# A hybrid decoder step on one core: warm-up products, another order of the first loads, bias tables in steps, and output weights prepared before the turn

## The chip, the cores and the metric

The kernel runs on one core of a Trainium2 chip. The metric is the device time of one execution in microseconds (us), as the median of the runs shown. A profile is one execution recorded by the hardware profiler. Engines are named as in the profile: PE is TensorE's matmuls and PEld its weight loads, DVE is VectorE, ACT is ScalarE, POOL is GpSimd, SP is SyncE, which issues nearly all DMAs.

## What is computed

One layer of a decoder for 512 prompt tokens and 32 new sample tokens (8 sequences of 4), 2048 channels, all in float32. In short:

```python
h = rms_norm(x, norm_pre)
z = h @ w_in                      # 2048 x 7680: q, k, v, gate_attn, conv a, conv b, gate_conv
att_p = attend_prompt(q, k, v)    # 12 heads x 128, three dilated windows, one relative bias table
att_s = attend_sample(q, k, v, cache_kv)   # 8 sequences, 2048 cached rows each
c = pointwise(silu(layer_norm(depthwise_conv(a * sigmoid(b)))))
mix = concat(att * silu(gate_att), c * silu(gate_conv))
y = x + rms_norm(mix @ w_out, norm_post)   # 2048 x 2048
```

The outputs are y, the new convolution states, the prompt's k and v, and the whole key and value cache shifted by 4 rows with the new rows behind (some 200 MB that are copied from DRAM to DRAM).

## The kernel before

**Splitting.** Each large product is made of three products of a faster float type: a value is split into a high half (a cast on ACT) and a low half (value minus high half, on POOL or DVE), and high x high, low x high and high x low are summed. A weight half is called wh or wl for the input projection and owh or owl for the output projection, x is split into xh and xl, and the mix into mh and ml.

**Input projection.** 60 column tiles of 128 columns are taken in a fixed order, `order`; n counts them. The 544 tokens are two halves of 272, so a tile is 16 x 2 x 3 = 96 products, written by `mm` at L107 into banks z. `project` (L849) makes a tile in four parts; each part calls `split` (L798) for weights that come two quarters later, and `split` calls `load_w` (L149) two half tiles ahead, into four buffers `raw`. After each part comes a `tick` (L767). As each half of a tile is done, `out` (L989) multiplies it by the token scale R on DVE; the gates' tanh and products follow the tile (L1034).

**First tiles.** The first NF = 3 tiles are made together by `project_first` (L879), row by row as x arrives: `prepare` (L908) splits x rows (`split_x`, L252) and weights (`split_first`, L886) one quarter ahead. R needs the sum of squares of each token: `square` (L271) on ACT from a second copy of x by tokens (`load_xtok`, L268; five blocks, the fifth holds the 32 last tokens), then `token_rsqrt` (L195) on ACT and DVE, and a product with a diagonal (rbx) that spreads it. `make_R` (L312) stands ahead of the last six rows of products.

**Bias tables.** `make_tabs` (L295) makes the relative bias tables by four products (tb, rb) that share one bank `s`, each followed by an ACT copy; the first pair goes to DRAM (dtab) and is read back for each head by `load_toep`. It is a generator: each `yield` is a step.

**Side work.** Attention of the heads, the samples' work and the convolution are generators, `Side` (L60), that `tick` advances in order of their rank: a yield gives the ticks until the next step. For the samples a key unit takes UTK ticks and a value unit UTV ticks (L44); there are 24 of each, and each unit loads 1.75 MB of cache (kvf, kvm) into buffers of two. `tick` also sends pending stores (`flush_late`) and issues copies of the cache (`bulk`, L321) while the bytes sent are below START + PACE x the columns that PE has been given so far (L46, L775).

**Order.** Each engine runs its instructions in the order of the program (`in_order`, L76), and SP issues in that order too: a load that waits for its buffer holds what is behind it.

**The turn.** After tile 59 come the gate of the last head, the samples' last gate (`ms`, L1064), the closing of the attention buffers, loads of gpost (gp) and of the samples' x, and then `split_mix` (L779) for the mix rows 2 to 15 (rows 0 and 1 were made at n = 57). The output projection (L1146) takes four groups of 512 columns, 16 rows each; a row is 3 products of 512 columns for each of two token blocks. `split_out` (L821) splits the output weights up to 6 rows ahead, with low halves on POOL, every third on DVE. The 32 sample rows go another way: `sample_rows` (L1131) multiplies the unsplit weights in `oraws` by the samples' mix `smix` (os, L109), four rows at a time.

```python
            if n == NF - 1:
                project_first(first)
                add(make_tabs(), 0, 0)
                now[0] += 8
                for _ in range(4):
                    tick()
...
    ms = mixg[2][:, :, SEQ:]
    nc.vector.scalar_tensor_tensor(ms, ms, 0.5, smp["sg"], op0=ALU.mult, op1=ALU.mult)
    ap_.close()
...
    nc.gpsimd.tensor_copy(smix[:, 8:12, :], ms)
    for i in range(NPRE, KT):
        split_mix(i)
```

Of the kernel before, what the change touches and what calls it, by code (L numbers as in the profile page):

```python
# [10 lines left out]
F32 = mybir.dt.float32  # L11
# [7 lines left out]
P = 128  # L19
# [23 lines left out]

UTK, UTV = 3.8, 3.7  # L44

# [40 lines left out]
def body(tc, xT, xtok, gpost, w_in, w_out, ckv, cconv, relb, vecs, pww, c_oht, c_ohr, c_lmr, c_tm, c_pick,  # L86
# [88 lines left out]
    epsc = keep.tile([P, 1], F32, name="epsc")  # L175
    dma(vec, vecs)
    make_identity(nc, ident)
    nc.vector.memset(epsc, EPS)
# [10 lines left out]
    ones = keep.tile([P, P], F32, name="ones")  # L189
    nc.vector.memset(ones, 1.0 / 2048)  # L190

    sumsq = keep.tile([P, 5], F32, name="sumsq")
    nc.vector.memset(sumsq, 1.0)

    def token_rsqrt(ss, pool):  # L195


        r, v, w = [pool.tile([P, 5], F32, name=n + "x") for n in "rvw"]
        diag = pool.tile([P, 5, P], F32, name="diagx")
        nc.scalar.activation(r, ss, AF.Sqrt, bias=epsc[:, 0:1], scale=1.0 / 2048)  # L200
# [40 lines left out]
    def load_x(c):  # L241
        xr = ip.tile([P, 2, TOK], F32, tag="xr", name=f"xr{c}", bufs=6)
        if c:
            dma(xr, xT[:, 2 * c:2 * c + 2, :])
        else:
            for j in range(2):
                dma(xr[:, j, :], xT[:, j, :])
        return xr
# [14 lines left out]


    def xt_of(b):
        return mixg[(b + 1) % 4].rearrange("p a b -> p (a b)")[:P if b < 4 else NS, :D]

# [550 lines left out]
    osplits, oraws = {}, {}  # L818
    due = []

    def split_out(j):  # L821
# [24 lines left out]
        if j % 4 == 3:  # L846
            due.append(j - 3)

    def project(n, hi, lo, out):  # L849
# [29 lines left out]
    def project_first(outs):  # L879
# [28 lines left out]
        def prepare(c):  # L908
            if c == 0:
                split_x(0)  # L910
                ws = [split_first(0, n) for n in range(NF)]
                split_x(1)
            else:
                split_x(2 * c)
                ws = [split_first(c, n) for n in range(NF)]
                split_x(2 * c + 1)
            return ws

        ws = prepare(0)
        for c in range(4):  # L920
            nxt = prepare(c + 1) if c < 3 else None
            if c == 2:
                square(0)
                load_xtok(4)
                square(1)
            if c == 3:
                for b in range(2, 5):
                    square(b)
            rows(c, ws, 0, 2)
            if c < 3:  # L930
                rows(c, ws, 2, 4)
            ws_, ws = ws, nxt
# [6 lines left out]
    def samples():  # L939
        got = iter(())  # L940
        for g in range(3):
# [5 lines left out]
            state["vdone"] = g  # L947


    nc.scalar.activation(sumsq[:, 0:1], epsc, AF.Sqrt)  # L950
    load_w(0)
    xrs[0] = load_x(0)
    load_w(2)
# [8 lines left out]
    xrs[7] = load_x(7)  # L962
    for b in range(4):
        load_xtok(b)
# [4 lines left out]
    for n in range(N_IN):  # L969
        c = order[n]  # L970
        kind, h = divmod(c, NH)
        if n == NF:
            ini.close()
            sample_open()
            load_far(0)
            load_mid(0)
# [12 lines left out]
        def out(hf, z, t_=t_, c=c, g=g if c < 3 * NH else None, hh=hh if c < 3 * NH else None, nm=nm, n=n):  # L989
            if n == N_IN - 1 and hf == 0:  # L990
                for j in range(4):
                    split_out(j)
            if c >= NH:
# [8 lines left out]
        if n < NF:  # L1002
            first.append(out)
            if n == NF - 1:
                project_first(first)
                add(make_tabs(), 0, 0)
                now[0] += 8
                for _ in range(4):
                    tick()
        else:  # L1010
            project(n, xh, xl, out)
        if n == NF + 1:
            load_toep(0)
# [3 lines left out]
        if n == N_IN - 3:  # L1017
            smix = ring["a"].tile([P, KT, NS], F32, name="smix")
            for g in (0, 1, 3):
                nc.gpsimd.tensor_copy(smix[:, 4 * g:4 * g + 4, :], mixg[g][:, :, SEQ:])  # L1020
            for i in range(NPRE):
                split_mix(i)
        if n == NF:
            add(samples(), 0, 1)
# [50 lines left out]
    nc.gpsimd.tensor_copy(smix[:, 8:12, :], ms)  # L1075
    for i in range(NPRE, KT):
        split_mix(i)
    NBLK = 5
# [15 lines left out]
    def take_out(c, b, z):  # L1094
# [13 lines left out]
        nc.vector.tensor_tensor(ys[b][:np_, cs], z[:np_, :], gp[:np_, cs], op=ALU.mult)  # L1108

    def finish(b):  # L1110
        np_ = P if b < 4 else NS
# [16 lines left out]
    OLOOK = 6  # L1128
    sz = {}

    def sample_rows():  # L1131

        while due:
            j0 = due.pop(0)
            c = j0 // KT
            if c not in sz:
                sz[c] = bank("acc", f"os{c}")
            for a in range(4):
                i = (j0 + a) % KT
                mm(sz[c][a * NS:a * NS + NS, :], smix[:, KORD[i], :], oraws.pop(j0 + a).rearrange("p a b -> p (a b)"),  # L1140
                   start=(i < 4), stop=(i >= KT - 4), tile_position=(0, a * NS))
            if (j0 + 4) % KT == 0:
                take_out(c, 4, sz[c])

    sample_rows()
    for c in range(4):  # L1146
        last = c == 3

        for bs in (((0, 1), (2,), (3,)) if last else ((0, 1), (2, 3))):
            tags = ("z", "z") if 0 in bs else ("att", "s") if 2 in bs else ("t",)  # L1150
            z = [bank(t, f"oz{c}_{b}") for b, t in zip(bs, tags)]
            for i in range(KT):
                j = c * KT + i

                for a in range(OLOOK + 1):
                    if (j + a) // KT == c or 0 not in bs and j + a < NSLOT + c * KT + i:
                        split_out(j + a)
                        sample_rows()
                wh, wl = osplits[j]
                for b, z_ in zip(bs, z):  # L1160
# [139 lines left out]
```

## Time and profile before

| | |
|---|---|
| median of 3 runs | 1174.95 us (1173.05 to 1175.88) |
| profiled execution, its own time | 1170.97 us |
| span of the profile (first to last instruction) | 1169.2 us |
| PE busy | 1137.5 us, 97% |
| mean granted TensorE clock | 0.990 |
| moved by DMA | 401.92 MB, mean 344 GB/s |

Times in the profile count from the start of the span. A line of the timeline gives start, length, engine, source line, operation with the names of what it writes and reads, the number of merged instructions (x), and in brackets how long the engine was idle before and what ended that. Products in `mm` all have line 107, so they are told apart by names: z is the input projection, oz the output projection, os the samples' rows, tb and rb the tables, rbx the token scale.

### The profile page before, as it was taken

How to read it: one execution, taken by the hardware profiler on the slowest of the kernel's cores; microseconds unless marked ns; L12 is line 12 of the kernel's file. 1: busy time of each engine (PE TensorE's matmuls, PEld its weight loads, DVE VectorE, ACT ScalarE, POOL GpSimd, SP SyncE). 2: the span in 40 equal slices, each digit the busy share in tenths (PEclk: the TensorE clock that was granted, in tenths of full speed). 3: DMA queues.
4: the chain of work that ended last, by engine and by line, in shares of the span. 5: the costliest groups of instructions: out<-in, count | busy, mean ns of one | idle time of the engine just before them, and what ended most of it. 6: DMA issues, size and time to landing. Idle time of an engine off the chain costs nothing.

```text
span 1169.2 us, 23598 instructions
## 1 busy us (share of the span) xinstructions
PE 1137.5 (97%) x9322; PEld 1029.4 (88%) x9322; DVE 674.0 (58%) x1997; ACT 378.1 (32%) x749; POOL 406.8 (35%) x353
## 2 busy tenths in 40 slices
PE   7899999999999999999999999999999999999996
PEld 7699999999999999999999999899999976776775
DVE  5209899599699988778233576994222243112136
ACT  5433333422123332331334333423222253223241
POOL 5043323344344333333322222334333445313130
PEclk9989999999999999999999999999999998999999
DMA  9899999999998998999998899889999968999966
GB/s 363 278 339 373 402 351 343 383 312 338 408 329 320 402 381 323 351 362 355 408 375 331 293 384 395 330 317 373 387 386 338 337 218 292 337 357 389 332 232 225
DMA packets 96083, 401.92 MB, mean 344 GB/s; under 512 B 15000, under 2 KB 17816, under 8 KB 89765
## 3 DMA queue, kind: packets, MB, share of 16 engines
q1 hardware_dynamic: 95972, 400.42, 93.6%
q8 instruction: 73, 1.20, 0.4%
q14 instruction: 38, 0.30, 0.1%
HBM read 388.65 MB, written 212.66 MB: 514 GB/s over the span
## 4 chain that ended last, share of the span: by engine, by line
PE 56%; DVE 2%; DMA 1%; issue 1%; POOL 0%; ACT 0%; SPq 0%; DVEq 0%; ACTq 0%; POOLq 0%
PE z L107 32%; PE oz L107 14%; PE o L109 3%; PE pwp L107 1%; PE os L109 1%; PE att L107 1%; DMA raw<-in_w_out_dram 1%; PE s L107 1%; PE t L113 1%; DVE qsc L628 1%; POOL owl L844 0%; PE kt L113 0%; PE pvar L107 0%; PE pm L107 0%; PE sn L109 0%
## 5 line engine op out<-in xcount | busy, mean ns | idle before, releaser
L107 PE MATMUL z<-xh,wh 128*128 128x272 f32 x1920 | 572.3, 298 | 8.7 <-ACT wh L894 7.6
L107 PE MATMUL z<-xh,wl 128*128 128x272 f32 x1920 | 555.0, 289 | 1.1 <-POOL wl L895 0.6
L107 PE MATMUL z<-xl,wh 128*128 128x272 f32 x1920 | 553.4, 288 | 0.0
L810 POOL TENSOR_TENSOR wl<-raw,wh 128x512 fp32r<-128x512 f32 x228 | 311.1, 1374 | 471.3 <-ACT wh L809 447.7
L107 PEld LDWEIGHTS z<-xh,wh 128*128 128x128 f32 x1920 | 363.6, 189 | 25.2 <-issue 11.0
L107 PEld LDWEIGHTS z<-xl,wh 128*128 128x128 f32 x1920 | 363.2, 189 | 1.6 <-issue 1.0
L107 PEld LDWEIGHTS z<-xh,wl 128*128 128x128 f32 x1920 | 363.0, 189 | 1.8 <-POOL wl L895 0.9
L809 ACT CAST wh<-raw 128x512 fp32r<-128x512 f32 x228 | 139.1, 617 | 181.4 <-PE z L107 106.4
L334 DVE TENSOR_TENSOR t<-z,R 128x272 f32<-128x272 f32 x96 | 42.0, 439 | 181.5 <-PE z L107 170.2
L628 DVE SCALAR_TENSOR_TENSOR qsc<-kvf,qb 128x128 f32<-128x128 f32 x288 | 125.6, 436 | 8.8
L628 DVE SCALAR_TENSOR_TENSOR qsc<-kvm,qb 128x128 f32<-128x128 f32 x288 | 112.4, 390 | 8.8
L442 DVE SCALAR_TENSOR_TENSOR mix<-up,vec,mix 128x512 f32<-128x512 f32 x120 | 107.6, 896 | 0.0
L107 PE MATMUL oz<-owl,mh 128*128 128x512 f32 x256 | 101.7, 397 | 3.7 <-POOL owl L844 3.7
L107 PE MATMUL oz<-owh,mh 128*128 128x512 f32 x256 | 103.4, 404 | 1.5 <-ACT owh L843 1.5
L107 PE MATMUL oz<-owh,ml 128*128 128x512 f32 x256 | 101.3, 396 | 0.0
L844 POOL TENSOR_TENSOR owl<-raw,owh 128x512 fp32r<-128x512 f32 x43 | 61.4, 1447 | 111.2 <-ACT owh L843 81.8
L107 PEld LDWEIGHTS oz<-owh,mh 128*128 128x128 f32 x256 | 48.5, 189 | 26.4 <-issue 8.4
L844 DVE TENSOR_TENSOR owl<-raw,owh 128x512 fp32r<-128x512 f32 x21 | 21.7, 1032 | 73.0 <-ACT owh L843 72.8
L107 PEld LDWEIGHTS oz<-owl,mh 128*128 128x128 f32 x256 | 48.7, 190 | 15.6 <-POOL owl L844 4.1
L843 ACT CAST owh<-raw 128x512 fp32r<-128x512 f32 x64 | 36.8, 618 | 78.3 <-DMA raw<-in_w_out_dram 69.4
L107 PEld LDWEIGHTS oz<-owh,ml 128*128 128x128 f32 x256 | 48.4, 189 | 10.6
L444 DVE SCALAR_TENSOR_TENSOR mix<-us,vec,mix 128x32 f32<-128x32 f32 x120 | 57.0, 475 | 0.0
(180 smaller groups left out, 991.7 us busy)
## 6 DMA issues: line engine op xcount, KB each, us to landing
out_dram<-in_ckv_dram SPq DMA_DIRECT2D x168, 1152.0 KB, 12.2
raw<-in_w_in_dram SPq DMA_DIRECT2D x119, 512.0 KB, 9.7
kvm<-in_ckv_dram SPq DMA_DIRECT2D x48, 1024.0 KB, 10.5
kvf<-in_ckv_dram SPq DMA_DIRECT2D x144, 256.0 KB, 8.2
raw<-in_w_out_dram SPq DMA_DIRECT2D x32, 512.0 KB, 9.1
out_dram<-t SPq DMA_DIRECT2D x24, 256.0 KB, 9.2
mix<-in_xtok_dram SPq DMA_DIRECT2D x4, 1024.0 KB, 14.0
xt<-in_xtok_dram SPq DMA_DIRECT2D x8, 512.0 KB, 4.7
```

What stands on the lines that cost most here:

```text
L107: nc.tensor.matmul(out, lhsT, rhs, start=start, stop=stop)
L109: nc.tensor.matmul(out, lhsT, rhs, start=start, stop=stop, tile_position=tile_position)
L113: nc.tensor.transpose(out, in_, eye)
L334: nc.vector.tensor_tensor(dst[:, sl], z[hf][:, :HT], R[:, sl], op=ALU.mult)
L442: nc.vector.scalar_tensor_tensor(cc[:, ct, :SEQ], up[:, j:j + SEQ], wj, cc[:, ct, :SEQ], op0=ALU.mult, op1=ALU.add)
L444: nc.vector.scalar_tensor_tensor(cs, us[:, :, j:j + NT], wj, cs, op0=ALU.mult, op1=ALU.add)
L628: nc.vector.scalar_tensor_tensor(scr, src[:, hh * P:hh * P + P], SCALE, qb[:, hh * P:hh * P + P], op0=ALU.mult, op1=ALU.mult, accum_out=sd ...
L809: nc.scalar.copy(wh, raw)
L810: nc.gpsimd.tensor_tensor(wl, raw, wh.bitcast(F32), op=ALU.subtract)
L843: nc.scalar.copy(wh, raw)
L844: (nc.vector if j % 3 == 2 else nc.gpsimd).tensor_tensor(wl, raw, wh.bitcast(F32), op=ALU.subtract)
```

## The change

1. UTK goes from 3.8 to 3.75 and UTV from 3.7 to 3.3.
2. Eleven products of the matrix `ones` with itself run at the start into an unused bank. The load of `vec` moves behind the first weight and the first x half; that x half is issued from ACT's queue; ACT's first activation comes after it. The first weight is split ahead of the first x rows. x has 5 load buffers instead of 6, and the diagonal uses one of them.
3. The 32 last tokens get a buffer of their own (xt4) and are loaded ahead of the other four blocks.
4. The first three quarters of tile NF are split in the last stage of `project_first`, between the squares and the token scale. The tables are added as a side that runs in the ticks of tile NF; the opening of the samples' buffers, their first loads and their start come one tile later.
5. `out` splits output weights 0 to 3 at n = 58 and 4 to 7 at n = 59, and runs `sample_rows` there. Mix rows 2 to 5 are split after tile 59, before the last gate; rows 6 to 15 one by one inside the first 10 rows of the output projection.

```diff
-UTK, UTV = 3.8, 3.7
+UTK, UTV = 3.75, 3.3
...
-    dma(vec, vecs)
-    make_identity(nc, ident)
...
+    make_identity(nc, ident)
+
+    warm = bank("t", "warm")
+    for _ in range(11):
+        nc.tensor.matmul(warm[:, 0:P], ones, ones, start=True, stop=True)
...
-        diag = pool.tile([P, 5, P], F32, name="diagx")
+        diag = pool.tile([P, 2, TOK], F32, tag="xr", name="diagx", bufs=5).rearrange("p a b -> p (a b)")[:, :5 * P]
+        diag = diag.rearrange("p (a b) -> p a b", a=5)
...
-        xr = ip.tile([P, 2, TOK], F32, tag="xr", name=f"xr{c}", bufs=6)
+        xr = ip.tile([P, 2, TOK], F32, tag="xr", name=f"xr{c}", bufs=5)
         if c:
             dma(xr, xT[:, 2 * c:2 * c + 2, :])
         else:
-            for j in range(2):
-                dma(xr[:, j, :], xT[:, j, :])
+            sent[0] += 4 * P * TOK
+            tc.keep_in_program_order(nc.scalar.dma_start(xr[:, 0, :], xT[:, 0, :]))
+            dma(vec, vecs)
+            dma(xr[:, 1, :], xT[:, 1, :])
...
+    xt4 = ip.tile([NS, D], F32, name="xt4")
+
     def xt_of(b):
-        return mixg[(b + 1) % 4].rearrange("p a b -> p (a b)")[:P if b < 4 else NS, :D]
+        if b == 4:
+            return xt4
+        return mixg[(b + 1) % 4].rearrange("p a b -> p (a b)")[:, :D]
...
             if c == 0:
+                ws = [split_first(0, 0)]
                 split_x(0)
-                ws = [split_first(0, n) for n in range(NF)]
+                ws += [split_first(0, n) for n in range(1, NF)]
...
                 square(0)
-                load_xtok(4)
                 square(1)
             if c == 3:
                 for b in range(2, 5):
                     square(b)
+                for a in range(3):
+                    split(4 * NF + a)
...
-
-    nc.scalar.activation(sumsq[:, 0:1], epsc, AF.Sqrt)
     load_w(0)
     xrs[0] = load_x(0)
+
+    nc.scalar.activation(sumsq[:, 0:1], epsc, AF.Sqrt)
...
-    for b in range(4):
+    for b in (4, 0, 1, 2, 3):
         load_xtok(b)
...
-        if n == NF:
+        if n == NF + 1:
             ini.close()
             sample_open()
             load_far(0)
...
-            if n == N_IN - 1 and hf == 0:
+            if n >= N_IN - 2 and hf == 0:
                 for j in range(4):
-                    split_out(j)
+                    split_out(j + 4 * (n - N_IN + 2))
+                sample_rows()
...
                 project_first(first)
-                add(make_tabs(), 0, 0)
-                now[0] += 8
-                for _ in range(4):
-                    tick()
+                add(make_tabs(), 11, 0)
+                now[0] += 12
         else:
             project(n, xh, xl, out)
+        if n == N_IN - 1:
+            for i in range(NPRE, NPRE + 4):
+                split_mix(i)
...
-        if n == NF:
+        if n == NF + 1:
             add(samples(), 0, 1)
...
-    for i in range(NPRE, KT):
-        split_mix(i)
...
-    sample_rows()
     for c in range(4):
...
                         split_out(j + a)
                         sample_rows()
+                if c == 0 and 0 in bs and i + NPRE + 4 < KT:
+                    split_mix(i + NPRE + 4)
```

The functions `sample_rows` and its list `sz` move ahead of `project` unchanged, but for names: `smix` and `take_out` are reached through the lists `smixs` and `take`.

## Rows read from the trace of the kernel before

**Rows 1.** The page, busy time of each engine, and the DMA share in 40 slices.

```profile
PE 1137.5 (97%) x9322; PEld 1029.4 (88%) x9322; DVE 674.0 (58%) x1997; ACT 378.1 (32%) x749; POOL 406.8 (35%) x353
...
DMA  9899999999998998999998899889999968999966
```

**Rows 2.** Table of stretches: us, busy us of PE, PEld, DVE, ACT, POOL (x instructions), granted clock, DMA share, GB/s.

```profile
7.60:13.53 5.93, 5.29 (x21) 4.97 (x22) 1.76 (x3) 3.06 (x5) 3.88 (x3) 1.00 1.01 403
...
42.40:45.70 3.30, 0.09 (x1) 0.00 (x0) 1.28 (x8) 1.88 (x3) 0.00 (x0) 1.00 1.13 447
...
51.75:59.40 7.65, 4.88 (x10) 0.84 (x8) 0.79 (x4) 2.46 (x6) 0.00 (x0) 0.69 0.37 116
...
59.40:64.80 5.40, 4.86 (x20) 4.54 (x21) 0.00 (x0) 1.52 (x3) 4.97 (x4) 0.50 0.84 266
...
64.80:74.20 9.40, 9.40 (x76) 9.40 (x76) 0.44 (x1) 2.06 (x4) 2.98 (x3) 1.00 1.08 439
...
961.40:967.40 6.00, 0.85 (x3) 0.30 (x2) 6.00 (x9) 4.80 (x10) 4.38 (x2) 0.88 0.54 176
...
967.40:972.70 5.30, 5.28 (x15) 2.53 (x16) 2.13 (x2) 0.58 (x2) 5.30 (x4) 0.50 0.48 145
```

**Rows 3.** PE's waits over the whole span: us in total, times, longest us.

```profile
PE z L107 <- ACT wh L894: 7.6, 1, 7.6
...
PE oz L107 <- POOL owl L844: 3.7, 1, 3.7
...
PE rbx L107 <- DVE diagx L208: 3.3, 1, 3.3
...
PE s L107 <- DVE pr L359: 2.1, 2, 1.4
```

**Rows 4.** Timeline of the first 20 us: start us, us, engine, line, work, [idle before <-releaser].

```profile
1.65 0.91 SPq L98 DMA_DIRECT2D xr<-in_xT_dram  x2
...
5.29 0.75 ACT L258 ACTIVATE xh<-xr,vec 128x544 fp32r<-128x544 f32 x1 [3.06 <-DMA xr<-in_xT_dram]
...
8.48 0.62 ACT L894 CAST wh<-raw 128x512 fp32r<-128x512 f32 x1 [0.91 <-DMA raw<-in_w_in_dram]
...
9.18 2.52 POOL L895 TENSOR_TENSOR wl<-raw,wh 128x512 fp32r<-128x512 f32 x2 [0.17 <-ACT wh L894]
```

**Rows 5.** Timeline, ScalarE and PE, 36 to 66 us.

```profile
41.98 1.91 ACT L273 ACTIVATE mix<-mix 32x2048 f32<-32x2048 f32 x1 [3.47 <-DMA mix<-in_xtok_dram]
...
44.01 0.30 ACT L200 ACTIVATE rx<-sumsq,epsc 128x5 f32<-128x5 f32 x1
...
45.79 1.52 PE L107 MATMUL rbx<-diagx,ones 128*128 128x128 f32 x12 [3.30 <-DVE diagx L208]
...
51.81 1.03 PE L107 MATMUL tb<-oht,rel 33*12 33x512 f32 x2
...
53.50 0.39 PE L107 MATMUL tb<-oht,rel 33*12 33x128 f32 x2 [0.66 <-ACT tabs L299]
...
54.23 1.71 PE L107 MATMUL rb<-ohr,lt 128*96 128x512 f32 x2 [0.34 <-ACT tabs L299]
```

**Rows 6.** The turn: timeline of ScalarE and VectorE, and GpSimd's line of tile owl, 953 to 980 us.

```profile
954.67 7.75 ACT L786 CAST mh<-mix 128x544 fp32r<-128x544 f32 x14
...
956.56 9.07 DVE L787 TENSOR_TENSOR ml<-mix,mh 128x544 fp32r<-128x544 f32 x14
...
L844 POOL TENSOR_TENSOR owl<-raw,owh x8: 1260/1510/4351, 963.0 to 976.0; 128x512 fp32r<-128x512 f32 x8
```

**Rows 7.** Timeline of SP's queue before the turn.

```profile
937.79 9.81 SPq L98 DMA_DIRECT2D raw<-in_w_out_dram  x2
```

**Rows 8.** The last value phase: PE's timeline, and landings of tile kvm.

```profile
808.54 0.86 PE L109 MATMUL o<-kvf,spt 128*32 128x128 f32 x24
...
823.60 0.86 PE L109 MATMUL o<-kvf,spt 128*32 128x128 f32 x24
...
DMA to landing us min/median/max: 7.6/8.6/11.4
```

More of the change, by code (lines that the diff above doesn't have):

```diff
@@ L818, in body @@
     osplits, oraws = {}, {}
-    due = []
+    due, take, smixs = [], [], []
     def split_out(j):
@@ L847, in split_out, with sample_rows @@
             due.append(j - 3)
+    sz = {}
+    def sample_rows():
+        while due:
+            j0 = due.pop(0)
+            c = j0 // KT
+            if c not in sz:
+                sz[c] = bank("acc", f"os{c}")
+            for a in range(4):
+                i = (j0 + a) % KT
+                mm(sz[c][a * NS:a * NS + NS, :], smixs[0][:, KORD[i], :], oraws.pop(j0 + a).rearrange("p a b -> p (a b)"),
+                   start=(i < 4), stop=(i >= KT - 4), tile_position=(0, a * NS))
+            if (j0 + 4) % KT == 0:
+                take[0](c, 4, sz[c])
     def project(n, hi, lo, out):
@@ L1018, in body @@
             smix = ring["a"].tile([P, KT, NS], F32, name="smix")
+            smixs.append(smix)
             for g in (0, 1, 3):
@@ L1108, in take_out @@
         nc.vector.tensor_tensor(ys[b][:np_, cs], z[:np_, :], gp[:np_, cs], op=ALU.mult)
+    take.append(take_out)
     def finish(b):
@@ L1128, in body @@
     OLOOK = 6
[L1129 to L1143, printed above, removed]
-    sample_rows()
     for c in range(4):
```

## The prediction

> **What bounds the kernel now.** I read the page first: PE is busy 97% of the span, and the DMA row stands at 9 nearly everywhere [rows 1]. So every microsecond that PE does not work, or works at half clock, is on the path, and a change that adds no PE work can win only there. Next I read the granted clock and PE's busy time stretch by stretch [rows 2]. At full clock a z product takes 9.40/76 = 0.124 us. (The first stretch reads 1.00 too, but 21 products took 5.29 us there, 0.25 each: half clock.) PE falls short of that in four places: before and around the first products (21 products in the 5.93 us to 13.53), at 42.4 to 45.7, at 51.75 to 64.8, and at the turn from the input to the output projection, 961.4 to 972.7. PE's list of waits [rows 3] names who ended each: ScalarE's first weights after 7.6 us, VectorE's diagonal after 3.3 us, GpSimd's output weights after 3.7 us. Last, I read the timeline of these four places [rows 4 to 7] for what was late. The reader should see that the middle, some 850 us, holds almost no wait: its largest entry is 2.1 us.
>
> **The start.** Before, the first cast waits in ScalarE's queue behind two x halves, and the first of those waits 3.06 us for its load [rows 4]; so GpSimd's first low half comes late too. After, weights and x come first, vec moves behind them, the first weight cast stands ahead of the x splits, and eleven warm products run meanwhile. Six products of that kind took 1.52 us at full clock [rows 5], so eleven at half take 11 x 0.51 = 5.6 us, inside the 7.6 us in which PE waits anyway: cost 0. The first tile's first 12 products should then be done before the second tile's weights land, which is at 8.48 as before (the bytes ahead of them are the same). From there loads rule: the third tile's low half is ready at 9.18 + 2.52 = 11.70 [rows 4], 12 products follow at 0.124, and 36 stand done at 13.2. Before, 21 were done at 13.53; the same moment now has 38, 17 x 0.124 = 2.1 us. I take 2.0. Bounds: if the clock stays low to 13.5 as before, the first 12 end by 9.2, the second tile's last ten, from 10.44 at 0.25, end near 13, and 25 or so are done: 0.5. If the weights come one issue (0.46 us, half of the row with two) sooner: 2.5.
>
> The first x half now goes out from ScalarE's queue. SP spends 0.91 us on its two halves [rows 4]. The Trainium skill ("DMA: Bandwidth & Descriptors", Issuing engines are not separate DMA queues) says that transfers from different queues run on the same engines and only the issue time is saved; no trace of before has a second queue. By that rule the term stays at 2.0; were the queue a path of its own, the second tile's weights would come sooner and it would be nearer 2.5.
>
> **Last tokens' sums.** Before, ScalarE is free at 41.98 - 3.47 = 38.51, then waits for the 32 last tokens, whose load was issued last; PE runs dry at 42.49 and resumes at 45.79 [rows 2, 5]. After, that load goes first and has its own tile. ScalarE runs 2.0 us earlier (its casts there wait for PE's buffers), so: 36.5, plus the square 44.01 - 41.98 = 2.03, plus the three new casts put ahead of the root, 3 x 0.62 = 1.86 [rows 4], plus root to product 45.79 - 44.01 = 1.78, gives 42.2. PE arrives at 40.5 and waits 1.7 instead of 3.3: **1.6**. What is late next is the root behind the casts. Bounds: 0, if the big token loads now end the squares no sooner; 3.3, if the casts fit beside it. One x buffer fewer delays the last two x loads by about one x split; they are used a tile's work later, so 0; without that cover, up to one split, 1.39 us, of the start term.
>
> **Tables in steps.** Before, 51.75 to 64.8 holds 20 z products and the tables [rows 2]: 13.05 - 20 x 0.124 = 10.6 us. The table products follow each other through one bank with ScalarE's copies between, then ScalarE casts and GpSimd subtracts, and only then does PE start, at half clock. After, casts and low halves of the fourth tile are made during the last rows, and the tables come in two steps between its products. They then cost 1.03 + 0.66 + 0.39 + 0.34 [rows 5], and the two rb products at full clock, half of 1.71 each, 1.7 in all: 4.1 us. Gain 6.5 if the clock stays. It did fall in this very sequence (mean 0.69 in that stretch), yet after 3.3 idle us at 42.4 it did not [rows 2]. If it falls again, 20 products cost 0.12 more each and rb its old time: 4.1 us, gain 2.4. I take **5.2**, nearer to no fall since dense products follow at once. Moved with it: two weight loads go ahead of cache copies on SP, the table's store waits for its step as it waited before, and the weights queued behind are for a tile later. The sample buffers open one tile later, when rb has run; their loads land in 7.6 to 11.4 us [rows 8], a tile takes 96 x 0.124 = 11.9, and VectorE, not PE, would meet a late one: 0.
>
> **The pace of the sample work.** It does the same work, starts 4 ticks later and takes 24 x (0.05 + 0.4) = 10.8 ticks less, so it ends some 7 ticks sooner, which the early output weights need. PE work is equal: 0. Bounds: 2.1 gained, if the middle's wait [rows 3] goes; 2 lost, if it comes twice.
>
> **The turn.** Before, 14 casts (7.75 us) and 14 subtractions (9.07 us) of the mix stand in ScalarE's and VectorE's queues ahead of the fifth output weight, and beside the latter a GpSimd subtraction takes 4351 ns instead of 1260 [rows 6]. PE idles 6.00 - 0.85 = 5.15 us, then runs 5.3 us at half clock [rows 2], of which 2.65 is lost: 7.8. After, eight output weights are split inside the last two tiles, four mix rows before the last gate, and ten one by one beside products. PE uses 6 x 0.23 = 1.4 us a row (a product of 512 columns costs 512/272 of 0.124), the queues a cast or two (0.62 each) and a subtraction: they keep ahead. The added wait: the four products on the raw weights now stand at the end of tile 58 and again of tile 59, ahead of the next tile on PE. Raw loads need slots that GpSimd frees: SP is held on two of them from 937.79 for 9.81 us, to 947.6 [rows 7]; the last tile ends near 953.5, so that load has 6 us. The four casts wait on loads too, with the gate's tanh behind them. I take 0.3 for this: **7.5**. Bounds: 1.5, if GpSimd's 3.7 us wait and the low clock stay; 7.8.
>
> **Sum:** 2.0 + 1.6 + 5.2 + 7.5 = 16.3 us. The profiled execution takes 1170.97 with a span of 1169.2, so 1154.7 for one like it; the median of the runs is 4 us above it, and I predict the median: 1174.95 - 16.3 = 1158.6. The low bounds add to 0.5 + 0 + 2.4 + 1.5 - 2 = 2.4, the high ones to 2.5 + 3.3 + 6.5 + 7.8 + 2.1 = 22.2; all at one end is unlikely.
>
> **Rivals.** (1) *The turn keeps its stall* (0.14): a raw load lands late and PE waits at the moved products, or GpSimd's subtractions still crawl beside VectorE's. For: the 4351 ns, and a held SP. Against: the early weights are subtracted inside tiles where VectorE has little to do. The turn gives 1.5: 1174.95 - 10.3 = 1164.6. The Trainium skill ("SBUF — State Buffer", Who interferes with whom) says that a VectorE operation with two inputs from SBUF and a GpSimd one that reads it exclude each other, the second to start waiting for the first. The row of 4351 ns agrees in direction; by that rule each late weight would wait behind one 0.7 us subtraction, not a row of them, and the forecast stands.
>
> (2) *Transfers set the pace* (0.06): the DMA row is at 9 [rows 1], and bytes follow PE's progress, so a PE that waits less only gets ahead of its loads. What is won early is given back in waits for raw weights. For: the row. Against: no DMA stands in PE's largest waits [rows 3], and the early idle stretches have DMA shares down to 0.37 [rows 2]. Most of it lost, it gives about 1173, no change.
>
> (3) *The quicker sample pace starves* (0.03, slower). In the value phase a unit takes 823.60 - 808.54 = 15.06 us at 3.7 ticks; at 3.3 it is 0.4 x 24 x 0.124 = 1.2 us shorter. Loads go out when a buffer comes free, two units ahead, and land in at most 11.4 us [rows 8], against about 27 us. It decides only if landings pass that; then 24 units waiting 1 us each outweigh 16.3: 1174.95 + 24 - 16.3 = 1182.7.
>
> (4) The warm products do nothing, since the clock falls again before the weights come: part of the forecast's own range (start 0.5: 1160.1).
>
> **Numbers.** The forecast has 0.77. Its own range is 1153 to 1163; reaching to rival 1 and to bad luck in two terms, 1152 to 1167. About 0.3%, 3.5 us, is what a measurement of this kernel can tell from no change; the forecast and rival 1 are both faster by more: 0.91, within it 0.06, slower 0.03.
>
> **What would show it.** Right: first dense products by 11 us and a z product at 0.124 well before 13.5; a wait of 1 to 2 us for the diagonal; no stretch without z products at 52 to 59; PE busy through the turn at clock 1.00. Wrong: half clock in the fourth tile, waits for raw loads at the end of tiles 58 and 59, new waits of PE in the middle, or a middle stretch whose z products no longer follow each other.

## The result and the profile after

The changed kernel takes **1162.21 us** (median of 4 runs, 1161.13 to 1163.06), the kernel before, run beside it, 1174.51 (1173.05 to 1175.88): a ratio of 0.9894, 95% interval 0.9879 to 0.9910. It is 12.3 us faster; the forecast was 1158.6, a gain of 16.3. The profiled execution of after takes 1162.85 us with a span of 1161.1, close to its median, while that of before (1170.97) is 3.5 us below the 1174.51, so the two profiles differ by 8.1 us only.

Where these 8.1 us lie can be read off by counting PE's products in the two timelines: z products are the same 5760 in the same order, so the start of the k-th (from 0) is the same point of the work in both.

| stretch | before, us | after, us | gained |
|---|---|---|---|
| start of the span to z 96 | 22.91 | 20.72 | 2.2 |
| z 96 to z 246 (six products ahead of the diagonal's) | 18.67 | 18.67 | 0 |
| z 246 to the end of z 287 (its start plus 0.124; the end of the first three tiles) | 10.13 | 14.93 | -4.8 |
| from there to z 384 (tables, fourth tile) | 22.74 | 16.17 | 6.6 |
| z 384 to z 5471 (the middle) | 842.34 | 844.76 | -2.4 |
| z 5471 to z 5663 | 24.49 | 24.06 | 0.4 |
| z 5663 to oz 64 (the turn) | 39.80 | 31.80 | 8.0 |
| oz 64 to oz 767 (the last) | 178.67 | 180.49 | -1.8 |

The loss in the third line is seen at once in the list of PE's waits of after (us in total, times, longest):

```profile
PE rbx L107 <- DVE diagx L212: 4.9, 1, 4.9
PE s L107 <- DVE pr L369: 1.9, 2, 1.7
PE os L109 <- DMA raw<-in_w_out_dram: 1.7, 1, 1.7
...
PE z L107 <- ACT srow L668: 0.8, 2, 0.7
PE z L107 <- POOL wl L921: 0.8, 1, 0.8
PE tb L107 <- ACT tabs L309: 0.7, 1, 0.7
```

The two waits of 7.6 us for the first weight and 3.7 us for the output weights [rows 3] are gone. The wait for the diagonal has grown from 3.3 to 4.9, and behind the diagonal the clock is low, as the table of stretches of after shows (us, busy us of PE, PEld, DVE, ACT, POOL with instructions, granted clock, DMA share, GB/s):

```profile
45.24:54.32 9.08, 9.08 (x48) 9.08 (x49) 2.73 (x11) 0.77 (x2) 0.00 (x0) 0.62 1.02 367
54.32:70.50 16.18, 15.17 (x107) 12.95 (x106) 1.26 (x5) 4.09 (x8) 4.51 (x4) 1.00 0.75 262
...
953.71:971.10 17.39, 17.39 (x84) 12.30 (x81) 15.38 (x18) 10.11 (x19) 9.47 (x7) 1.00 0.91 329
```

The first line holds the diagonal's products and the last z products of the first tiles at a mean clock of 0.62; in the second, the fourth tile and the tables run at 1.00, where before they stood at 0.69 and 0.50 [rows 2]; the third is the turn, with PE busy all the time at 1.00. The timeline of after, all engines, shows why the diagonal is late (start, us, engine, line, work, count, idle before and what ended it):

```profile
33.69 1.92 ACT L283 ACTIVATE mix<-mix 128x2048 f32<-128x2048 f32 x1 [0.47 <-DMA mix<-in_xtok_dram]
...
38.10 1.90 ACT L283 ACTIVATE xt<-xt 32x2048 f32<-32x2048 f32 x1
39.99 1.64 ACT L819 CAST wh<-raw 128x512 fp32r<-128x512 f32 x3
40.67 3.70 POOL L820 TENSOR_TENSOR wl<-raw,wh 128x512 fp32r<-128x512 f32 x3 [10.74 <-DMA ohr<-in_c_ohr_dram]
41.54 0.29 ACT L204 ACTIVATE rx<-sumsq,epsc 128x5 f32<-128x5 f32 x1
41.86 0.19 DVE L206 RECIPROCAL rx<-rx 128x5 f32<-128x5 f32 x1 [1.58 <-ACT rx L204]
42.09 1.08 DVE L207 TENSOR_TENSOR wx<-rx 128x5 f32<-128x5 f32 x1
43.20 1.19 DVE L208 TENSOR_TENSOR wx<-wx,vx 128x5 f32<-128x5 f32 x1
44.42 0.17 DVE L209 TENSOR_SCALAR wx<-wx 128x5 f32<-128x5 f32 x1
45.24 2.74 PE L107 MATMUL rbx<-diagx,ones 128*128 128x128 f32 x12 [4.94 <-DVE diagx L212]
```

Two things stand between the last square and the product. The root at 41.54 waits behind three casts. Two VectorE steps on five columns take 1.08 and 1.19 us while GpSimd subtracts three weights (40.67 to 44.37), and the next, when GpSimd is done, takes 0.17 again. Ahead of both, squares of the token blocks waited for their loads (0.50, 0.47 and 0.49 us at 31.22, 33.69 and 36.19). These loads are later than before. SP's queue, before and then after:

```profile
14.44 4.25 SPq L98 DMA_DIRECT2D mix<-in_xtok_dram  x4
```
```profile
13.28 2.34 SPq L98 DMA_DIRECT2D xr<-in_xT_dram  x2
15.67 0.42 SPq L98 DMA_DIRECT2D xt<-in_xtok_dram  x1
16.15 3.79 SPq L98 DMA_DIRECT2D mix<-in_xtok_dram  x4
```

The four large blocks (mix) go out 1.7 us later, behind x loads that wait for one of five buffers (SP waits 3.2 us for these up to 24 us, 0.3 before) and behind the 32 last tokens (xt). The second block landed at 29.1 before and at 31.2 after, the third at 31.6 and 33.7. The product then takes 2.74 us in place of 1.52 [rows 5]: the clock has fallen.

The turn came out as meant. PE's timeline of after has the samples' products of the last tile and the first output products with no wait between, and GpSimd's low halves, done in time, take 1.3 to 1.4 us each:

```profile
952.72 1.06 PE L109 MATMUL os<-raw,smix 128*32 128x512 f32 x8
953.71 0.50 PE L107 MATMUL oz<-owh,mh 128*128 128x512 f32 x1
```
```profile
935.76 4.24 POOL L854 TENSOR_TENSOR owl<-raw,owh 128x512 fp32r<-128x512 f32 x3
945.22 3.81 POOL L854 TENSOR_TENSOR owl<-raw,owh 128x512 fp32r<-128x512 f32 x3
```

### The profile page after: what moved, and what is told of

It is laid out like the page before. It is cut to its first block, busy times and chain, and to the rows that moved or that the text cites. A ratio compares the mean times of both kernels' runs of the same rounds, so it can differ in the third digit from the quotient of the medians.

```text
span 1161.1 us, 23634 instructions
## 1 busy us (share of the span) xinstructions
PE 1137.1 (98%) x9344; PEld 1031.5 (89%) x9344; DVE 681.5 (59%) x1997; ACT 377.2 (32%) x749; POOL 402.0 (35%) x353
## 4 chain that ended last, share of the span: by engine, by line
PE 85%; DMA 6%; DVE 5%; ACT 1%; issue 1%; SPq 1%; DVEq 0%; ACTq 0%
PE z L107 56%; PE oz L107 13%; PE o L109 4%; DMA raw<-in_w_out_dram 3%; DVE qsc L638 2%; PE att L107 2%; PE s L107 2%; DMA mix<-in_xtok_dram 1%; PE pwp L107 1%; DMA raw<-in_w_in_dram 1%; PE t L113 1%; PE os L109 1%; DMA xr<-in_xT_dram 1%; PE qbp L113 1%; PE kt L113 1%
## 5 line engine op out<-in xcount | busy, mean ns | idle before, releaser
L638 DVE SCALAR_TENSOR_TENSOR qsc<-kvf,qb 128x128 f32<-128x128 f32 x288 | 119.1, 414 | 8.8
L638 DVE SCALAR_TENSOR_TENSOR qsc<-kvm,qb 128x128 f32<-128x128 f32 x288 | 119.2, 414 | 8.6
L452 DVE SCALAR_TENSOR_TENSOR mix<-up,vec,mix 128x512 f32<-128x512 f32 x120 | 103.7, 864 | 0.0
L854 POOL TENSOR_TENSOR owl<-raw,owh 128x512 fp32r<-128x512 f32 x43 | 58.7, 1381 | 108.7 <-ACT owh L853 108.2
L454 DVE SCALAR_TENSOR_TENSOR mix<-us,vec,mix 128x32 f32<-128x32 f32 x120 | 59.7, 498 | 0.0
## 6 DMA issues: line engine op xcount, KB each, us to landing
out_dram<-in_ckv_dram SPq DMA_DIRECT2D x168, 1152.0 KB, 11.9
```

What stands on the lines that cost most here:

```text
L452: nc.vector.scalar_tensor_tensor(cc[:, ct, :SEQ], up[:, j:j + SEQ], wj, cc[:, ct, :SEQ], op0=ALU.mult, op1=ALU.add)
L454: nc.vector.scalar_tensor_tensor(cs, us[:, :, j:j + NT], wj, cs, op0=ALU.mult, op1=ALU.add)
L638: nc.vector.scalar_tensor_tensor(scr, src[:, hh * P:hh * P + P], SCALE, qb[:, hh * P:hh * P + P], op0=ALU.mult, op1=ALU.mult, accum_out=sd ...
L854: (nc.vector if j % 3 == 2 else nc.gpsimd).tensor_tensor(wl, raw, wh.bitcast(F32), op=ALU.subtract)
```

## The experiments

Twelve kernels ran, each compared with the kernel before on the same chip (1174.34 beside the first four, 1174.79 and 1174.69 beside the others). Between the groups the kernel before differs by 0.5 us at most, so medians of different groups are set side by side. The question was what made the diagonal late, and which parts of the change give and take.

**1. Early splits behind the token scale.**

```diff
             if c == 3:
                 for b in range(2, 5):
                     square(b)
-                for a in range(3):
-                    split(4 * NF + a)
...
         make_R()
+        for a in range(3):
+            split(4 * NF + a)
         rows(3, ws_, 2, 4)
```

> The changed kernel, with the three early weight splits of the fourth tile moved behind the token scale. Theory A (the three casts, 1.64 us on ScalarE, and GpSimd's subtractions beside VectorE's small operations are what makes PE wait for the diagonal): the wait falls from 4.9 to about 1.5 us, the clock stays at 1.00 between 40 and 55 us, the 36 products behind it run at 0.124 instead of about 0.2; 3.4 us plus some 3 us, so about 1155.5 us. Theory B (one x buffer fewer and the later token loads make it): the wait stays above 3.3 us and the time within 1.5 us of 1162.

Measured: 1159.13 us, ratio 0.9868 (0.9853 to 0.9883), 3.1 us below the changed kernel (the intervals touch), less than the 6.7 of theory A. Its timeline, root to product:

```profile
40.05 0.30 ACT L204 ACTIVATE rx<-sumsq,epsc 128x5 f32<-128x5 f32 x1
...
40.61 0.17 DVE L207 TENSOR_TENSOR wx<-rx 128x5 f32<-128x5 f32 x1
40.81 0.17 DVE L208 TENSOR_TENSOR wx<-wx,vx 128x5 f32<-128x5 f32 x1
...
41.83 1.52 PE L107 MATMUL rbx<-diagx,ones 128*128 128x128 f32 x12 [2.06 <-DVE diagx L212]
```

The root follows the last square, the two steps are short, and the product is at full clock. From its start to the end of the first tiles it took 5.93 us in place of 9.08. So the splits made most of the loss. A wait of 2.06 us is left: here too the squares wait for their loads, four times 0.4 to 0.5 us. And part of the gain was given back: in this execution the clock fell later, at the tables (54 to 58 us at 0.56 and 0.59), and the fourth tile took 17.65 us in place of 16.17.

**2. PE kept busy in the gap** by 16 products ahead of the token scale:

```diff
+        for _ in range(16):
+            nc.tensor.matmul(warm[:, 0:P], ones, ones, start=True, stop=True)
         make_R()
```

> The changed kernel with 16 products of the matrix ones (0.25 us each at full clock, 4 us) put on PE in the wait for the diagonal; the wait itself is not shortened. Theory A (half of what the wait costs is the clock that falls in it): the clock stays at 1.00 behind it, and 36 products that took half clock are made at 0.124: 3 to 4 us less, about 1158.5 us. Rival (the clock falls in the profiled execution alone, not in the timed ones): no change, 1162 us.

Measured: 1161.62 us, 0.9887 (0.9874 to 0.9901): no gain that can be told. The products ended at 43.5, the token loads came 1.1 us later in this execution, PE still waited 2.85 us, and the clock was 0.80 and 0.50 behind it all the same. Against experiment 8, whose loads came as late and which has no filling, z 246 to the end of the first tiles takes 14.84 us in place of 15.12. It doesn't say what a longer filling would do.

**3. One warm-up product in place of eleven.**

```diff
-    for _ in range(11):
-        nc.tensor.matmul(warm[:, 0:P], ones, ones, start=True, stop=True)
+    nc.tensor.matmul(warm[:, 0:P], ones, ones, start=True, stop=True)
```

> The changed kernel with one warm-up product instead of eleven. Theory A (the warm-up raises the clock before the first z products, but loads rule most of the start): the first z product still near 5.8 us, products at 0.25 until about 12 us, rows done at 14 us fewer by about 10: 1 to 1.5 us slower, 1163.5 us. Rival (the warm-up carries the whole 2.2 us of the start): 1164.5 us. Rival (it carries nothing): 1162 us.

Measured: 1162.94 us, 0.9892 (0.9878 to 0.9906), the same as the change. The first z products start 0.226 us apart here and 0.124 with the eleven, yet z 96 starts at 21.06 against 20.72 in after, and 20.11 to 20.61 in experiments 1, 2, 6, 8 and 9, whose code is that of after up to there. So the warm-up is worth 0.3 to 1.0 us, with one execution on the side without it. The rest of the start's gain is left, by difference, for the order of loads and casts; no run has that alone.

**4. The turn alone**, on the kernel before (the diff's lines of `split_out`, `sample_rows` and `split_mix`, nothing else).

> The kernel before with the turn's part alone (output weights 0 to 7 split in the last two tiles, their sample rows there, mix rows spread). Theory A (the turn is worth what the profile of after shows at its end, 7.8 us): 1174.5 - 7.8 = 1166.7 us, PE busy and clock 1.00 through the turn. Rival (part of it is given back in the output projection in waits for raw weights, 1.5 us as after): 1168.2 us.

Measured: 1168.11 us, 0.9933 (0.9919 to 0.9947): 6.2 us between the medians, 7.9 by the ratio. The first fits the rival, the second theory A, so the time does not decide between them. In its trace z 5663 to oz 64 takes 31.81 us, as in the changed kernel, and oz 64 to oz 767 takes 180.65 against 178.67 in the profile of before. Up to the fourth tile this kernel is the one before, and here its clock did fall behind a wait of 3.0 us for the diagonal (0.50 from 46 to 50 us), where in the profile of before it had not behind 3.30 [rows 2, 5].

**5. The 32 last tokens loaded last again**, into their own tile, on experiment 1:

```diff
-    for b in (4, 0, 1, 2, 3):
+    for b in range(5):
         load_xtok(b)
```

> The changed kernel with the early splits behind the token scale (as in the first run of that kind, 1159.1), and with the 32 last tokens loaded last of the five blocks again, still into their own tile. Theory (the load of 32 rows ahead of the four large ones makes each of these land late: three squares waited 0.47 to 0.50 us each in the changed kernel): the squares run without waits, the wait for the diagonal falls from 2.06 to about 1 us, about 1158. Rival (the four large loads are late from the bytes ahead of them, whatever their order): squares wait as before, the diagonal 2 us, 1159. Other way round (it is the last square that waits, as before the change, by up to 3.5 us): the diagonal 3 us or more, 1160.5.

Measured: 1156.77 us, 0.9839 (0.9823 to 0.9854), 2.4 below experiment 1, though the intervals touch. Three squares have no wait, the fourth waits 1.60 us, the diagonal 1.42. The second and third block land at 29.2 and 31.7, where they landed before the change (29.1 and 31.6), though only five x buffers are left: it is the 32 tokens ahead of them that made these late. Over all fourteen profiles the second block lands at 30.4 to 32.3 us with the 32 tokens first and at 28.7 to 29.6 with them last. But the fourth block is late in either order.

**6. The tables in four steps**, one product pair each, on experiment 1:

```diff
-        dma_late(dtab, tabs, 2)
-        yield
+            if c0:
+                dma_late(dtab, tabs, 2)
+            yield
...
-                add(make_tabs(), 11, 0)
+                add(make_tabs(), 12, 0)
```

> The changed kernel with the early splits behind the token scale, and the tables in four steps of one product pair each in place of two steps of two. Theory (the second product of a pair waits for ScalarE's copy of the first, 0.7 and 0.3 us, and the clock that fell to 0.56 and 0.59 at 54 to 58 us fell behind these waits): both waits go, the clock stays nearer to 1.00 there, 1 to 3 us, about 1157. Rival (tables cost their own products' time and the clock falls by itself): no change, 1159.

Measured: 1157.85 us, 0.9852 (0.9839 to 0.9866), 1.3 below experiment 1, with intervals that overlap. No table product waits any more, and the fourth tile takes 14.95 us in place of 17.65. But this time the clock had fallen at the diagonal, behind a wait of 3.0, and z 246 to z 384 takes 26.40 us against 26.54 in experiment 1: that the steps themselves gain more than their two waits isn't shown.

**7. The pace alone**, on the kernel before:

```diff
-UTK, UTV = 3.8, 3.7
+UTK, UTV = 3.75, 3.3
```

> The kernel before with only the two pace numbers changed (3.75 and 3.3 ticks a unit). Prediction's term 0: the same time as before, 1174.3. Rival (the 2 us that the middle lost after the change, in waits of PE on VectorE's pr and on ScalarE's srow, come from the quicker pace): 1176.3. Other rival (it starves on loads): 1180 or more.

Measured: 1175.93 us, 1.0010 (1.0000 to 1.0019): 1.1 us slower, at the edge of what can be told. In its trace z 384 to z 5471 takes 844.42 us against 842.34 [before] and 844.76 [after]. PE's waits from 75 to 905 us, before and then this run:

```profile
PE s L107 <- DVE pr L359: 2.1, 2, 1.4
PE pa L113 <- ACT sde L668: 0.3, 1, 0.3
```
```profile
PE s L107 <- DVE pr L359: 1.7, 1, 1.7
PE pwp L107 <- ACT srow L658: 0.6, 1, 0.6
PE z L107 <- DVE mix L997: 0.5, 1, 0.5
PE z L107 <- POOL wl L810: 0.5, 1, 0.5
```

The pace shifts which sample work falls beside which tile, and the waits are others, 3.5 us in sum against 2.4. PE also runs a few more instructions in this stretch (7736 against 7731) and fewer in the next. The middle's loss belongs to the pace: it takes 842.31 to 842.43 us in the three profiles with the old pace (before, experiments 4 and 12) and 844.42 to 845.09 in the ten with the new one.

**8. Only GpSimd's early subtractions moved in the program**, behind the token scale; casts as in the change.

```diff
-                    split(4 * NF + a)
+                    split(4 * NF + a, later=True)
...
         make_R()
+        lower()
```

(`later` makes the cast only and keeps the subtraction in a list, `lower` issues those.)

> The changed kernel with the three early casts where they are, ahead of the root on ScalarE, and only their three subtractions on GpSimd moved behind the token scale. Theory (it is GpSimd's subtractions that hold VectorE's small steps between root and diagonal: 1.08 and 1.19 us beside them in place of 0.17): VectorE's two steps take 0.17 again, the wait for the diagonal falls from 4.9 to about 3 us, and the time to about 1160.5. Rival (the casts ahead of the root make the wait): wait over 4 us, 1162.

Measured: 1161.93 us, 0.9889 (0.9874 to 0.9904), no change. The edit did nothing: GpSimd's queue was empty, so the subtractions started with their casts as before (41.76 to 45.46), VectorE's steps again took 1.08 and 1.19, and with token loads 1.1 us later the wait was 6.15. It tells nothing apart.

**9. The same three subtractions on VectorE**, behind the diagonal in its queue:

```diff
-                    split(4 * NF + a)
+                    split(4 * NF + a, later=True)
...
         make_R()
+        lower(nc.vector)
```

(Here `lower` issues them on the engine given.)

> The changed kernel with its three early casts ahead of the root as they are, and the three early subtractions given to VectorE, behind the diagonal in its queue, in place of GpSimd (moving them in GpSimd's own queue had no effect, since that queue stood empty and they started with their casts as before). Theory (GpSimd's subtractions hold VectorE's steps of two inputs, and the casts hold the root, each a share): VectorE's two steps take 0.17 us in place of 1.08 and 1.19, the wait for the diagonal is about 3 us in place of 4.9 with token loads as in the changed kernel's profile, and the time 1159.5 to 1161. Rival (something else slows VectorE there, such as the token loads): the two steps stay over 0.5 us, 1162.

Measured: 1159.56 us, 0.9865 (0.9846 to 0.9885), 2.7 below the change (the intervals touch). Timeline:

```profile
40.42 1.64 ACT L826 CAST wh<-raw 128x512 fp32r<-128x512 f32 x3
41.96 0.29 ACT L204 ACTIVATE rx<-sumsq,epsc 128x5 f32<-128x5 f32 x1
...
42.51 0.17 DVE L207 TENSOR_TENSOR wx<-rx 128x5 f32<-128x5 f32 x1
42.71 0.17 DVE L208 TENSOR_TENSOR wx<-wx,vx 128x5 f32<-128x5 f32 x1
...
43.73 2.77 PE L107 MATMUL rbx<-diagx,ones 128*128 128x128 f32 x12 [3.94 <-DVE diagx L212]
```

With GpSimd still, the two steps take 0.17 each: it was its subtractions that held them. Root to product is 1.77 us in place of 3.70. The casts remain: the root comes 3.44 us after the square's start, as in the change, against 2.02 in experiment 1. So the splits cost 1.9 us by GpSimd and 1.4 by the casts.

**10. Experiments 1, 5 and 6 together.**

> The changed kernel with the early splits behind the token scale, the 32 last tokens loaded last into their own tile, and the tables in four steps. Theory (the two gains stand in different places: tile 4 and the wait for the diagonal): no wait at the tables, 1.4 to 2 us for the diagonal, tile 4 in 15 us, about 1155.5, below both 1156.8 and 1157.9. Rival (the clock falls once in this stretch whichever wait is taken away): 1157 to 1158.

Measured: **1155.57 us** (1155.25 to 1157.95), 0.9839 (0.9818 to 0.9860): faster than both kernels, 19.1 us below before and 6.6 below the change. By the ratio it equals experiment 5, so that the table steps add to that one isn't shown by the times. Stretches of it, the diagonal's product to the end of the first tiles, and the fourth tile with the tables:

```profile
42.13:49.65 7.52, 7.52 (x48) 7.52 (x49) 2.67 (x11) 2.33 (x5) 3.79 (x3) 0.77 1.04 371
49.65:64.61 14.96, 14.96 (x106) 12.89 (x105) 1.54 (x6) 2.98 (x6) 3.98 (x4) 1.00 0.98 319
```

The tables now cost 14.96 - 96 x 0.124 = 3.1 us and no wait. The diagonal waited 2.26 us (ScalarE waited 2.06 for one token block), and the clock fell there.

**11. The same with another pace**, 3.8 and 3.5 ticks.

> The kernel of the run beside it (e10) with 3.8 ticks for a key unit and 3.5 for a value unit, in place of 3.75 and 3.3; the samples then end where they did before the change, which the early output weights still allow. Theory (the quicker pace costs 1 to 2 us in the middle, where two rows of the attention wait for VectorE and for ScalarE): about 1154. Rival (those waits come from where the sample rows fall, by chance, and another pace has others): within 1 us of e10, either side.

Measured: 1157.01 us, 0.9850 (0.9829 to 0.9870), not to be told from experiment 10. In its profile the start is the best of all (diagonal waits 0.70, the clock stays at 1.00, z 384 at 61.72 against 64.61), and the middle the worst: 848.65 us against 845.09. PE's waits from 75 to 905 us sum to 6.1 us in place of 3.5. So the theory fails and the rival's cause stands, if not its bound of 1 us: each pace has its own waits, and the number in the change is not simply too quick.

**12. The last tokens' part alone**, on the kernel before: own tile, loaded first, five x buffers, the diagonal in one of them; the splits stay where they were.

```diff
-                load_xtok(4)
...
-    for b in range(4):
+    for b in (4, 0, 1, 2, 3):
         load_xtok(b)
```

> The kernel before with only the last tokens' part of the change: their own tile, loaded ahead of the other four blocks, five x buffers, the diagonal in one of them; no early splits. Theory (without casts and subtractions beside the root the part does what the prediction said, and more): the square of the last tokens ends by 40.5 us, the wait for the diagonal falls from 3.3 to 1.0 to 1.5 us, about 1172. Rival (the four large loads are late in their place): squares wait 0.5 us each, the diagonal 2 to 2.5 us, 1173.5 to 1174.5.

Measured: 1169.67 us, 0.9955 (0.9938 to 0.9971): 5.0 us faster, more than the 2.7 expected. In its timeline no square waits and PE doesn't wait for the diagonal at all:

```profile
36.95 1.90 ACT L278 ACTIVATE mix<-mix 128x2048 f32<-128x2048 f32 x1
38.84 1.90 ACT L278 ACTIVATE xt<-xt 32x2048 f32<-32x2048 f32 x1
...
42.76 1.42 PE L107 MATMUL rbx<-diagx,ones 128*128 128x128 f32 x12
```

The four large blocks are issued from about 16 us on here and in the changed kernel alike, and the second lands at 30.8 here, at 31.2 there. Here ScalarE comes to its first square at 31.27, and each block is in by its turn; in the change it comes at 28.72, since the start is 2.2 us shorter, and runs into them.

## Why the prediction was right or wrong

**Direction, range and the mechanism of three terms (start, tables, turn) held; the last tokens' term failed, and the pace lost 2 us.** By the two profiles the sum is off by half, 8.1 us against 16.3. That the median lies in the range, 0.8 us from its end, is in part luck: the terms were worked against a profile quicker than its median, and taken off the median.

*Start*: 2.0 predicted, 2.2 in the profiles (z 96 starts at 23.23 and 23.09 in experiments 4 and 7, which start as before did, so 2.2 is the low end). The warm products gave 0.3 to 1.0 of it (experiment 3), so rival 4 was in part true of them, and yet not of the term: the rest is left for the order of casts and loads. With one x half issued from ScalarE's queue, the second tile's first cast came at 8.38 against 8.48 [rows 4], as the forecast had it.

*Last tokens' sums*: +1.6 predicted, -4.8 in the profiles. Three steps of the sum were wrong. "ScalarE runs 2.0 us earlier ... so: 36.5, plus the square 2.03" put the last square's end at 38.5; it ended at 40.0, since three squares waited 1.46 us together for blocks that landed 2.1 us later than before. The prediction moved the 32 tokens ahead of them and put nothing for what this does to them; experiment 5 undoes the order, and the second and third land as before. That is the bound "if the big token loads now end the squares no sooner", taken as an end of the range and not as the case. Then "plus root to product 1.78" was taken from before, where GpSimd stood idle; with the three subtractions that the same change puts beside it, it is 3.70. The Trainium skill ("SBUF — State Buffer", Who interferes with whom) states that a VectorE operation with two inputs from SBUF contends with a GpSimd one that reads it, and that this is an exclusive lock. The trace agrees in the end times (the two steps end at 43.17 and 44.39, the second and third subtraction at 43.15 and 44.37) and in the 0.17 of experiment 9. The prediction weighed that at the turn, where PE lost nothing to it, and not here. The casts, 1.86 predicted, took 1.55 (39.99 to 41.54). Third, the wait was priced as idle time alone: behind 4.9 us (1 to 2 was the sign of being right) the clock was at 0.50, and the rest of the first tiles took 9.08 us in place of the 5.92 of before. In sum 42.2 was predicted for the product, 45.24 measured: 1.5 for the blocks, 1.9 for VectorE, less 0.3 for the casts; the low clock adds 3.2. The buffer that went did delay the last two x loads, by 1.5 us (13.28 against 11.81), and cost z 96 to z 246 nothing, as predicted.

Experiment 12 shows that the part by itself gives 5.0 us. What failed is the part in its company: beside the quicker start the later blocks are no longer in when ScalarE comes, and the early splits stand in the chain.

*Tables in steps*: 5.2 predicted, 6.6 in the profiles; the bound 6.5 is met, because the clock stayed at 1.00; where it fell there, in experiment 1, the fourth tile took 17.65 us, a gain of 5.1. The tables cost 16.17 - 11.9 = 4.3 us in the fourth tile, 4.1 predicted. Experiment 6 shows that two of the waits that the sum kept, 0.7 and 0.3 us, could go too.

*Pace*: 0 predicted, a loss of 2.4 in the profiles and 1.1 in the medians (experiment 7), about the bound of 2 given, but not by its cause. The wait for VectorE's pr did not come twice (1.9 us in sum against 2.1); new ones came, for ScalarE's srow 1.4 us in after, and PE's waits in the middle grew from 2.4 to 3.5. That is half of the loss; for the other half there is only the work that moved between this stretch and the next, which gives 0.4 back. These new waits in the middle were among the prediction's signs of being wrong.

*Turn*: 7.5 predicted, 8.0 in the profiles, 6.2 to 7.9 alone (experiment 4). Rivals 1 to 3 did not come: no GpSimd row over 1.8 us, raw loads not missing at the end of tiles 58 and 59, no starving samples. In the output projection PE then waited 1.7 us for a raw weight, near 1060 us. That need not be the change's doing: the runs that leave the turn as it was show such a wait too (1.3 us in experiment 7, 1.0 in experiment 12), and the profile of before happened to have little of it (0.2). Over all profiles oz 64 to oz 767 takes 178.67 to 179.85 us with the old turn and 178.80 to 180.88 with the new.

*The two baselines*: the working went against a profile in which the clock did not fall at the diagonal. In two other executions of that code (experiments 4 and 7) it fell: z 264 started at 51.27 and 50.01 against 48.73, and z 246 to the end of the first tiles took 12.69 and 11.82 against 10.13. Against these the last tokens' term is -2.2 and -3.1 in place of -4.8, which goes some way to a gain of 12.3 in the medians against 8.1 between the profiles. How often it falls was not measured.

## What to carry to other kernels

When work is moved to a place where an engine is idle, list what else runs there: a short chain of small operations that PE waits for had better not have casts ahead of it in its queue (1.4 us here), nor GpSimd's subtractions beside VectorE's steps of two inputs (1.9 us). And list what stands behind a load that is moved forward in a queue. Gains along one chain need not add up: what an earlier stage saves is only kept if the loads behind the next wait come early enough. And check with a second execution whether the profile that the sum is made against is a typical one.

## What the runs showed of the hardware

A VectorE operation on 5 columns with two inputs took 1.08 and 1.19 us beside GpSimd subtractions of 512 columns (1.26 us each) and 0.17 without them, on the same operands (experiment 9). The reciprocal, with one input, took 0.19 beside them and without.

The granted clock fell to 0.50 (1.2 GHz) behind PE waits of 2.26 us (experiment 10), 3.0 (4 and 6), 3.4 (7) and 4.9 (after), and stayed at 1.00 (2.4 GHz) behind 2.06 (experiment 1) and 3.30 (before). Before and experiments 4 and 7 run the same code up to there, so the wait by itself doesn't decide it. Where it fell, the products from the diagonal's to the end of the first tiles took 1.5 to 3.2 us longer than the 5.92 of before. In experiments 1 and 5 it stayed at the diagonal and fell at the tables, in 6 and 10 the other way round, in 4 and 7 it fell at both, and in 11 at neither.

The token blocks landed up to 1.1 us apart between executions of code that is the same up to there (last square at 38.10 in after, 39.19 in experiment 8), which is as much as some of the terms weighed here.
